# A hybrid decoder layer on one core: the order of sampled tokens' state steps, the spacing of the second up set, and a feature-major last quarter

## The chip, the cores and the metric

The kernel runs on one core of a Trainium2 chip. The core has a matrix engine (TensorE, PE in the profile, with its weight loads as PEld), a vector engine (VectorE, DVE), an activation engine (ScalarE, ACT), a general engine (GpSimd, POOL) and a queue that issues transfers (SyncE, SP). Each works through its own instructions in order; between engines there are semaphores. The metric is the time of one execution on the device in microseconds. Before the change it has a median of 1743.32 us in three runs (1743.06 to 1748.29).

## The reference, cut to what matters

One layer for 1024 new tokens and 8 sampled tokens (one each for 8 sequences with stored state), width 1024, all in float32:

- A norm, and one input projection of 6672 columns, split into queries, forget gates, values and gates of a gated recurrence with 8 heads (HGRN2), and gate z, x/B/C and time steps of a state-space mixer with 16 heads (Mamba-2).
- HGRN2 by chunks; the mixer by chunks of 128 with a state of 64 x 128 a head. For a sampled token the stored state is decayed, `S = S * exp(A dt) + (dt x) B`, and read, `y = S C + D x`.
- Both are normed, gated, joined and multiplied by `w_out`, and added to x.
- A norm, `w_up` to 2 x 2816 columns, a causal convolution of width 3 on the gate half, `silu(gate) * val`, `w_down`, added to x. A last norm follows:

```python
gate, val = jnp.split(h @ w['w_up'], 2, axis=-1)
x = x + (jax.nn.silu(gate) * val) @ w['w_down']
y = rmsnorm(x, final_norm_w)
```

Returned are the normed outputs, both recurrent states of both groups, and the convolution states.

## The kernel before, in words

Every large product is made of three matmuls: each operand is split into a rounded part (`hi`) and the rest (`lo`), and hi x hi, hi x lo and lo x hi are added up in PSUM. A split is a cast on ScalarE and a difference on VectorE, for weights (L199 and L201, L1443 and L1444) as for activations (L1344 and L1345).

Activations lie feature-major: 128 features on the partitions, tokens along the row. Weights are loaded by SP some tiles ahead. The PSUM pool "mm" has three banks, the pool "mx" four, and there is one "nx".

The order of TensorE's instructions is written out by hand up to the last round of the down product: a list of jobs (one weight tile each: `f`, `q`, `v`, `sg`, `z`, `x`, `o`) is driven one matmul at a time (`step`, `tick`), and smaller work is put between them. `after(n, work)` issues work n ticks later, `spread(pieces, n)` issues one piece every n ticks. On the other engines a planner sets the order: it takes what is ready by its own estimate of times, and of several ready instructions the one issued first in the program. Each engine then runs the planned order, whatever the true times are. `tc.issue_after(ins)` makes an instruction stand behind `ins` on its engine.

Three places matter here.

The state-space mixer: `drive(ssd(1), ...)` runs the second half of the heads beside jobs up to `v0`. `ssd_back` ends a chunk with the state's update on VectorE (L611), and `ssm_state_out` (L633) transposes the last state on TensorE (L636), copies it on VectorE (L638) and stores it. Later, at the beginning of the jobs z4, z5 and z6, `ssm_decode(0, i)` (L656) makes two half steps for the sampled tokens of one pair of heads: SP loads B, C and the stored state Sd, ScalarE scales Sd (L669, four instructions), VectorE makes the product with B (L670) and adds it (L671), SP stores it, POOL multiplies by C (L673), VectorE reduces (L674). Before z4 come the four jobs of head 0, `f0`, `q0`, `v0`, `sg0`, whose PSUM tiles ScalarE evicts at L926. The buffers of Sd (two, tag "ld") and of B and C (four, tag "d") are used by head 0 next (L959 to L964).

The up product: instead of the plain product, each up tile takes seven products of half depth (p1 to p7) on combinations of the blocks of activations and of weights (a Strassen-Winograd scheme). The tokens come as two sets, `usets[0]` and `usets[1]`. `set_of(1)` (L1320) builds the second: its pieces are splits (`put`) and combinations (`comb`, on VectorE or POOL, L1352), issued one every 6 ticks while the first up tile's products run on set 0. It pauses until every feature tile has been weighed (`weigh`, ScalarE, L1257). The norm's factor is applied to products later; `set_norm` computes it (L736 to L739) with a PSUM bank of "mx" for one of its parts. `up_load(j)` loads the weights of up tile j, `up_sums(j)` makes their four sums (POOL, L1424), `up_split` splits them. For j = 1 the sums are made only when `set_of(1)` has issued its combinations, and stand on POOL behind the last of them. `Up` evicts the products: ScalarE copies p1 and p5, VectorE adds p2, p4, p6, p7 and p3, POOL makes two differences after p7 (L1479, L1480).

The end: the last two tiles of the down product are done for quarters of the tokens in the order 3, 0, 1, 2. Quarters 3, 0 and 1 are feature-major: eight products of six matmuls (`down`), added to x on VectorE (L1688), then for each block of 128 tokens eight transposes into two "fin" banks of "mx" (L1695), the squares on ScalarE (L1697), the root, and two scalings with the last norm's weight (ScalarE L1704 and POOL L1705 for one half, VectorE L1707 for the other). Quarter 2 is token-major (`last_blocks`, L1657): activations are the stationary operand, the last weights the moving one, 512 wide, the products land in "fin" banks as tokens x features, and x is added by matmuls with the identity on its split halves, which `halved` (L1627) prepares.

Of the kernel before, what the change touches and what calls it, by code (L numbers as in the profile page):

```python
# [16 lines left out]
P = 128  # L17
# [33 lines left out]
def hybrid_layer(  # L51
# [578 lines left out]
    def h64(t):  # L630
        return t.rearrange("p (h q) -> p h q", q=64)

    def ssm_state_out(g):  # L633
        ps = bank("sT")
        for i in range(4):
            PE.transpose(ps[:, i * P:(i + 1) * P], S[g][:, i * P:(i + 1) * P], ident)  # L636
        so = half("so")
        V.tensor_copy(so, ps)  # L638
        SP.dma_start(ssm_prompt[0, 0, g * 8:(g + 1) * 8].rearrange("(i h) p n -> (h p) i n", h=2),
                     so.rearrange("p (i n) -> p i n", n=P))  # L640

    def d4(t):
        return t.rearrange("p (b n) -> p b n", n=P)

    def cb(t):
        return t.unsqueeze(2).to_broadcast([P, 4, P])
# [9 lines left out]
    def ssm_decode(g, i):  # L656
        j = g * 4 + i
        xdd = small.tile([P, 2, ND], F32, tag="xdd", name=nm("xdd"))
        xdec = xdk[:, j, :]
        V.tensor_tensor(xdd[:, 0, :], xdec, ddb[:, 0, j, :], op=ALU.mult)  # L660
        for b0 in (0, 4):
            bs = slice(b0, b0 + 4)
            Bb, Cb = tl("d", "Bb")[:, :512], tl("d", "Cb")[:, :512]
            for t_, r in ((Bb, 2 * g), (Cb, 2 * g + 1)):
                fetch(t_, bc_d[r, bs].rearrange("b n -> (b n)").unsqueeze(0).to_broadcast([P, 512]))
            Sd = tl("ld", "Sd")
            fetch(d4(Sd), state_ssm[0, bs, 2 * j:2 * j + 2].rearrange("b h p n -> (h p) b n"))
            for b in range(4):
                A.activation(d4(Sd)[:, b, :], d4(Sd)[:, b, :], AF.Copy, scale=ddb[:, 1, j, b0 + b:b0 + b + 1])  # L669
            V.tensor_tensor(d4(Bb), d4(Bb), cb(xdd[:, 0, bs]), op=ALU.mult)  # L670
# [243 lines left out]
    def head_in(h):  # L914
        t = {}

        def f_end():
            f, k = t["f"], tl("big" if h else "e", "k")
            A.activation(f[:, :NT], f[:, :NT], AF.Identity, bias=lbt2[:, 0, h:h + 1], scale=lbt2[:, 1, h:h + 1])
            V.tensor_scalar(k[:, :NT], f[:, :NT], -1.0, 1.0, op0=ALU.mult, op1=ALU.add)  # L920
            t["k"] = k

        for n, off, func in (("f", OFF_F, AF.Tanh), ("q", OFF_Q, AF.Silu), ("v", OFF_I, AF.Copy),
                             ("sg", OFF_G, AF.Silu)):
            def evict(c, cs, ps, n=n, func=func):
                A.activation(t[n][:, cs], ps, func, scale=0.5 if n == "f" else 1.0)  # L926
# [388 lines left out]
        mm(ps[:, :QW], ones, rst[:, cs])  # L1315
        rstd_of(rst[:, cs], tl("us", "nt"), ps[:, :QW], DM)

    usets, combed = [{}, {}], [None]

    def set_of(i):  # L1320

# [26 lines left out]
        def comb(out, eng, x_, y_, op):  # L1348
            t = quads(tl("x5", "sm")[:, :NT])
            out.append(t)  # L1350
            for q in range(2):
                combed[0] = eng.tensor_tensor(t[:, 2 * q:2 * q + 2], x_[q], y_[q], op=op)  # L1352
                yield

        def two(t):
# [21 lines left out]
            after(76, lambda: up_split(0, 1))  # L1377
        else:
            d_ = []
            yield from put("p1", a1, "hT")  # L1380
            yield from comb(d_, G, a1, b1, ALU.subtract)
            while len(weighed) < KT:
                yield
            yield from put("p2", a2, "big")
            yield from put("p4", b2, "big")
            yield from comb(s_, V, b1, b2, ALU.subtract)
            yield from comb(s_, V, two(s_[0]), a1, ALU.subtract)
            yield from comb(s_, G, two(s_[1]), a2, ALU.add)
            up_sums(1, combed[0])
            yield from put("p6", [s_[1]], "hT")  # L1390
            yield from put("p5", [s_[0]], "hT")
            yield from put("p7", d_, "hT")
# [7 lines left out]
    def up_load(j):  # L1400
        ws = []
        for c0 in (0, DFF):
# [4 lines left out]
            last_w[0] = SP.dma_start(t.rearrange("p (k m) -> p k m", m=P),  # L1407
                                     w_up[0, :, c0 + j * P:c0 + (j + 1) * P].rearrange("(k p) m -> p k m", p=P))
            ws.append(t)
        wparts[j] = ws  # L1410
        if j != 1:
            up_sums(j)

    def up_sums(j, behind=None):

        (g1, g2), (v1, v2) = ((t[:, :512], t[:, 512:]) for t in wparts[j])
        sums = {}

        def add(name, x_, y_):
            sums[name] = tl("t", "wt")  # L1420
            with ExitStack() as order_:
                if behind is not None:
                    order_.enter_context(tc.issue_after(behind.ins))
                (G if j else V).tensor_tensor(sums[name], x_, y_, op=ALU.add)  # L1424
            return sums[name]

        p7 = add("p7", v1, v2)
# [114 lines left out]
    with tc.manual_schedule(engines={mybir.EngineType.PE}):  # L1542
# [6 lines left out]
            tick()  # L1549
        up_split(0, 2)  # L1550
        up_split(0, 3)
        after(4, lambda: spread(set_of(1), 6))
        after(93, lambda: (set_norm(1, 0), set_norm(1, 1)))
        for _ in ups(0, [(name, i) for i in range(2) for name in FIRST]):
            tick()
# [63 lines left out]
    for k in range(nk):  # L1619
# [5 lines left out]
    halves_ = []  # L1625

    def halved():  # L1627
        identr = tl("us", "idr", F32R)[:, :P]
        A.copy(identr, ident)
        halves_.append(identr)  # L1630
        for h4 in range(2):
            hi, lo = tl("x5", "xfh", F32R)[:, :1024], tl("x5", "xfl", F32R)[:, :1024]
            halves_.append((hi, lo))
            for m in range(4):
                x_, at_ = xT[4 * h4 + m][:, quarters[2]], slice(m * 256, (m + 1) * 256)
                A.copy(hi[:, at_], x_)
                V.tensor_tensor(lo[:, at_], x_, hi[:, at_].bitcast(F32), op=ALU.subtract)
                yield

    def summed(b):  # L1640
        t0 = quarters[2].start + b * P
        tb = [bank("fin"), bank("fin")]
        for i in range(2):
            ds, first_ = slice(i * 512, (i + 1) * 512), True
            for k in range(nk):
                for a, x in ((0, 0), (1, 0), (0, 1)):
                    mm(tb[i], acts[k][a][:, t0:t0 + P], wd[k][x][:, ds], start=first_, stop=k == nk - 1 and x == 1)
                    tick()
                    if first_:
                        first_ = False  # L1650
                        for m in range(4):
                            for x_ in halves_[1 + i]:
                                mm(tb[i][:, blk[m]], x_[:, m * 256 + b * P:m * 256 + (b + 1) * P], halves_[0],
                                   start=False, stop=False)
        return t0, tb

    def last_blocks():  # L1657
        for b in range(2):
            t0, tb = summed(b)
            ss = keep.tile([P, 4], F32, tag="ss", bufs=4, name=nm("fss"))  # L1660
            ot, sq = ([tl("t", "ot") for _ in range(2)] for _ in range(2))
            for i in range(2):
                ds = slice(i * 512, (i + 1) * 512)
                A.activation(sq[i], tb[i], AF.Square, accum_out=ss[:, i:i + 1])
                V.tensor_tensor(ot[i], tb[i], fw[:, ds], op=ALU.mult)
            V.tensor_tensor(ss[:, 2:3], ss[:, 0:1], ss[:, 1:2], op=ALU.add)
            A.activation(ss[:, 3:4], ss[:, 2:3], AF.Sqrt, bias=epsc, scale=1.0 / DM)
            V.reciprocal(ss[:, 3:4], ss[:, 3:4])
            for i in range(2):
                if i:  # L1670
                    A.activation(ot[i], ot[i], AF.Copy, scale=ss[:, 3:4])
                else:
                    V.tensor_scalar(ot[i], ot[i], ss[:, 3:4], None, op0=ALU.mult)
                SP.dma_start(y_prompt[0, t0:t0 + P, i * 512:(i + 1) * 512], ot[i])

    for c in (3, 0, 1, 2):
        cs = quarters[c]
        if c == 2:
            for _ in split_:
                pass  # L1680
            last_blocks()
            break
        if c == 0:
            split_ = halved()
            spread(split_, 3)
        for m in range(KT):
            ps = down(lambda k: wd[k], nk, slice(m * P, (m + 1) * P), acts, c)
            V.tensor_tensor(xT[m][:, cs], xT[m][:, cs], ps, op=ALU.add)  # L1688
        for t0 in range(cs.start, cs.stop, P):
# [10 lines left out]
            V.reciprocal(ss[:n, 3:4], ss[:n, 3:4])  # L1700
            for i in range(2):
                ds = slice(i * 512, (i + 1) * 512)
                if i:
                    A.activation(ot[i][:n], tb[i][:n, :], AF.Copy, scale=ss[:n, 3:4])  # L1704
                    G.tensor_tensor(ot[i][:n], ot[i][:n], fw[:n, ds], op=ALU.mult)  # L1705
                else:
# [33 lines left out]
```

## Time and profile before

| | |
|---|---|
| median of three runs | 1743.32 us |
| profiled execution, its time | 1742.79 us |
| its span, first to last instruction | 1741.1 us |
| TensorE busy | 1705.4 us, 98% of the span |
| VectorE, ScalarE, POOL busy | 1089.1, 789.8, 483.4 us |
| mean granted clock of TensorE | 0.997 |

Rows of the timeline give the start and the duration in us, the engine, the line of the kernel, the operation and its tiles (out<-in). In brackets stands how long the engine was idle before it and what ended that. A row "A <- B: t, n, m" of the waits says that A waited for B for t us in n waits, the longest m. Rows of stretches give, for A:B us, the length, each engine's busy time with its count, the granted clock, the DMA share and GB/s.

### The profile page before, as it was taken

The page shows a single profiled execution, that of the slowest core. Times are in us where ns is not written, and L with a number is a line of the kernel's source. Part 1 is how long each engine was busy: PE and PEld are TensorE (multiplying, and loading weights), DVE is VectorE, ACT ScalarE, POOL GpSimd, SP SyncE. Part 2 cuts the span into 40 slices and gives each one's busy share as a digit, 9 for nine tenths or more (in the row PEclk, how much of TensorE's full clock was granted, in tenths as well). Part 3 has the DMA queues.
Part 4 walks back from the last instruction along what each step waited for, and adds up shares of the span by engine and source line. Part 5 has one row for each costly group of instructions (what it writes and reads, how often), then busy time and mean ns, then how long its engine had stood idle before and what let it go on. Part 6 is the DMA issues. An engine that isn't in the chain of part 4 may idle for free. (4 is left out here: it accounts for less than half of the span.)

```text
span 1741.1 us, 38505 instructions
## 1 busy us (share of the span) xinstructions
PE 1705.4 (98%) x16111; PEld 1656.5 (95%) x16111; DVE 1089.1 (63%) x1983; ACT 789.8 (45%) x1441; POOL 483.4 (28%) x501
## 2 busy tenths in 40 slices
PE   7999999999999999999999989999999999999998
PEld 7999999999999999999999989999999999999997
DVE  6668666555565565567746777667676668544454
ACT  7677686344454354545334554333344334111124
POOL 2102131110120122011222266666666664000002
PEclk9999999999999999999999999999999999999999
DMA  5354334633434425335347712222222226322212
GB/s 165 73 123 120 96 91 144 186 103 105 130 94 120 115 88 142 118 99 178 119 145 252 230 53 87 97 74 74 74 80 80 97 75 240 138 90 77 86 44 98
DMA packets 250212, 200.22 MB, mean 115 GB/s; under 512 B 48020, under 2 KB 221574, under 8 KB 250022
## 3 DMA queue, kind: packets, MB, share of 16 engines
q1 hardware_dynamic: 249750, 197.67, 37.2%
q8 instruction: 126, 2.06, 0.5%
q14 instruction: 48, 0.39, 0.1%
q0 software_dynamic: 288, 0.10, 0.0%
HBM read 155.16 MB, written 46.95 MB: 116 GB/s over the span
## 5 line engine op out<-in xcount | busy, mean ns | idle before, releaser
L93 PE MATMUL mm<-hl,wh 128*128 128x344 f32 x1248 | 405.5, 325 | 0.0
L93 PE MATMUL mm<-hh,wh 128*128 128x344 f32 x1248 | 405.0, 325 | 0.0
L93 PE MATMUL mm<-hh,wl 128*128 128x344 f32 x1248 | 402.0, 322 | 0.0
L93 PEld LDWEIGHTS mm<-hl,wh 128*128 128x128 f32 x1248 | 235.4, 189 | 4.8 <-issue 4.2
L93 PEld LDWEIGHTS mm<-hh,wh 128*128 128x128 f32 x1248 | 235.4, 189 | 3.4 <-issue 2.8
L93 PEld LDWEIGHTS mm<-hh,wl 128*128 128x128 f32 x1248 | 235.6, 189 | 1.4 <-issue 1.2
L199 ACT CAST wh<-ws 128x1024 fp32r<-128x1024 f32 x96 | 100.6, 1048 | 238.8 <-PE dn L93 125.8
L93 PE MATMUL ub<-uh,wh 128*128 128x258 f32 x704 | 199.7, 284 | 4.1 <-DVE nt L737 3.3
L93 PE MATMUL ub<-uh,wl 128*128 128x258 f32 x704 | 198.9, 283 | 0.0
L93 PE MATMUL ub<-ul,wh 128*128 128x258 f32 x704 | 198.3, 282 | 0.0
L93 PE MATMUL dn<-ah,wh 128*128 128x256 f32 (+1 forms) x640 | 180.6, 282 | 1.1 <-DVE x L1611 1.1
L93 PE MATMUL dn<-al,wh 128*128 128x256 f32 (+1 forms) x640 | 180.2, 282 | 0.0
L93 PE MATMUL dn<-ah,wl 128*128 128x256 f32 (+1 forms) x640 | 179.7, 281 | 0.0
L201 DVE TENSOR_TENSOR wl<-ws,wh 128x1024 fp32r<-128x1024 f32 x88 | 115.3, 1310 | 81.0 <-ACT wh L199 81.0
L93 PE MATMUL ua<-uh,wh 128*128 128x258 f32 x528 | 149.6, 283 | 2.6 <-DVE val L1506 1.3
L93 PE MATMUL mm<-mh,wh 128*128 128x258 f32 x512 | 146.3, 286 | 4.9 <-DVE x L1233 4.1
L93 PE MATMUL ua<-uh,wl 128*128 128x258 f32 x528 | 149.3, 283 | 0.1
L93 PE MATMUL ua<-ul,wh 128*128 128x258 f32 x528 | 148.7, 282 | 0.0
L93 PE MATMUL mm<-ml,wh 128*128 128x258 f32 x512 | 145.1, 283 | 0.0
L93 PE MATMUL mm<-mh,wl 128*128 128x258 f32 x512 | 144.7, 283 | 0.0
L93 PEld LDWEIGHTS ub<-uh,wh 128*128 128x128 f32 x704 | 133.0, 189 | 4.5 <-DVE nt L737 3.5
L1444 DVE TENSOR_TENSOR wl<-wt,wh 128x512 fp32r<-128x512 f32 x88 | 89.6, 1037 | 75.1 <-ACT wh L1443 75.0
(394 smaller groups left out, 3982.5 us busy)
## 6 DMA issues: line engine op xcount, KB each, us to landing
ws<-in_w_in_dram SPq DMA_DIRECT2D x52, 512.0 KB
ws<-in_w_up_dram SPq DMA_DIRECT2D x44, 512.0 KB
ws<-in_w_out_dram SPq DMA_DIRECT2D x24, 512.0 KB
act_d<-val SPq DMA_DIRECT2D x22, 516.0 KB
al<-act_d SPq DMA_DIRECT2D x22, 516.0 KB
ws<-in_w_down_dram SPq DMA_DIRECT2D x22, 512.0 KB
ml<-mix_d SPq DMA_DIRECT2D x48, 172.0 KB
csb<-cs_d SPq DMA_DIRECT2D x32, 256.0 KB
```

The source lines that it names most:

```text
L93: PE.matmul(out, lhsT, rhs, start=start, stop=stop)
L199: A.copy(wh[:, :n], ws[:, :n])
L201: V.tensor_tensor(wl[:, :n], ws[:, :n], wh[:, :n].bitcast(F32), op=ALU.subtract)
L1444: V.tensor_tensor(lo[:, cs], sums[name], hi[:, cs].bitcast(F32), op=ALU.subtract)
```

## The change

Four things are changed. `ssm_decode`'s product with B stands on VectorE behind the newest copy of a state (`freed[0]`), and its scaling on ScalarE behind the newest eviction of a head's job (`freed[1]`). At the beginnings of z4, z5 and z6 these are the copy of the second state, L638, and the third eviction of `sg0`. In `set_of(1)` the d combination comes ahead of the p1 splits, the p4 splits come behind the combinations, and a piece is issued every 4 ticks instead of 6. The sums of up tile 1 are made by `up_load`, like all others, with no place given on POOL. Quarter 2 at the end is done like the other three; for it alone both halves are scaled on VectorE. `halved`, `summed` and `last_blocks` go.

```diff
-        V.tensor_copy(so, ps)
+        freed[0] = V.tensor_copy(so, ps)
...
             for b in range(4):
-                A.activation(d4(Sd)[:, b, :], d4(Sd)[:, b, :], AF.Copy, scale=ddb[:, 1, j, b0 + b:b0 + b + 1])
-            V.tensor_tensor(d4(Bb), d4(Bb), cb(xdd[:, 0, bs]), op=ALU.mult)
+                with tc.issue_after(freed[1].ins):
+                    A.activation(d4(Sd)[:, b, :], d4(Sd)[:, b, :], AF.Copy, scale=ddb[:, 1, j, b0 + b:b0 + b + 1])
+            with tc.issue_after(freed[0].ins):
+                V.tensor_tensor(d4(Bb), d4(Bb), cb(xdd[:, 0, bs]), op=ALU.mult)
...
-                A.activation(t[n][:, cs], ps, func, scale=0.5 if n == "f" else 1.0)
+                freed[1] = A.activation(t[n][:, cs], ps, func, scale=0.5 if n == "f" else 1.0)
...
+            yield from comb(d_, G, a1, b1, ALU.subtract)
             yield from put("p1", a1, "hT")
-            yield from comb(d_, G, a1, b1, ALU.subtract)
             while len(weighed) < KT:
                 yield
             yield from put("p2", a2, "big")
-            yield from put("p4", b2, "big")
             yield from comb(s_, V, b1, b2, ALU.subtract)
             yield from comb(s_, V, two(s_[0]), a1, ALU.subtract)
             yield from comb(s_, G, two(s_[1]), a2, ALU.add)
-            up_sums(1, combed[0])
+            yield from put("p4", b2, "big")
             yield from put("p6", [s_[1]], "hT")
...
-        wparts[j] = ws
-        if j != 1:
-            up_sums(j)
-
-    def up_sums(j, behind=None):
-
-        (g1, g2), (v1, v2) = ((t[:, :512], t[:, 512:]) for t in wparts[j])
+        (g1, g2), (v1, v2) = ((t[:, :512], t[:, 512:]) for t in ws)
...
-        after(4, lambda: spread(set_of(1), 6))
+        after(4, lambda: spread(set_of(1), 4))
...
     for c in (3, 0, 1, 2):
         cs = quarters[c]
-        if c == 2:
-            for _ in split_:
-                pass
-            last_blocks()
-            break
-        if c == 0:
-            split_ = halved()
-            spread(split_, 3)
...
-                if i:
+                if i and c != 2:
                     A.activation(ot[i][:n], tb[i][:n, :], AF.Copy, scale=ss[:n, 3:4])
                     G.tensor_tensor(ot[i][:n], ot[i][:n], fw[:n, ds], op=ALU.mult)
                 else:
```

More of the change, by code (lines that the diff above doesn't have):

```diff
@@ L631, in h64 @@
         return t.rearrange("p (h q) -> p h q", q=64)
+    freed = [None, None]
     def ssm_state_out(g):
@@ L1316, in set_norm @@
         rstd_of(rst[:, cs], tl("us", "nt"), ps[:, :QW], DM)
-    usets, combed = [{}, {}], [None]
+    usets = [{}, {}]
     def set_of(i):
@@ L1351, in comb @@
             for q in range(2):
-                combed[0] = eng.tensor_tensor(t[:, 2 * q:2 * q + 2], x_[q], y_[q], op=op)
+                eng.tensor_tensor(t[:, 2 * q:2 * q + 2], x_[q], y_[q], op=op)
                 yield
@@ L1420, in add @@
             sums[name] = tl("t", "wt")
[L1421 to L1424, printed above, removed]
+            (G if j else V).tensor_tensor(sums[name], x_, y_, op=ALU.add)
             return sums[name]
@@ L1624, in hybrid_layer @@
         wd.append((hi, lo))
[L1625 to L1669, printed above, removed]
-                if i:
[L1671 to L1674, printed above, removed]
```

1 line of the change is left out of this document (removed).

## The prediction

> **What bounds the kernel now.** I read the page first, then TensorE's own waits, and then the timeline of all queues around the longest of them.
>
> ```profile
> span 1741.1 us, 38505 instructions
> PE 1705.4 (98%) x16111; PEld 1656.5 (95%) x16111; DVE 1089.1 (63%) x1983; ACT 789.8 (45%) x1441; POOL 483.4 (28%) x501
> ```
>
> TensorE is busy for 1705.4 of 1741.1 us, so 35.7 us are left, and the start and the last stores take part of those. An edit can gain only where TensorE stands still or where it takes matmuls away. Its waits, as receiver, releaser, total, count and longest:
>
> ```profile
> PE ub L93 <- DVE nt L737: 3.3, 1, 3.3
> PE sT L636 <- DVE S L611: 2.4, 1, 2.4
> PE fin L93 <- ACT ot L1704: 1.7, 1, 1.7
> PE ua L93 <- DVE val L1506: 1.3, 1, 1.3
> PE ua L93 <- DVE us L1478: 1.0, 1, 1.0
> PE ub L93 <- ACT us L1474: 0.8, 1, 0.8
> ```
>
> Each of the three longest stands in one of the three places that the diff touches. So the question is, place by place, whether the edit takes the wait away and what is late next.
>
> **Part A, sampled tokens beside z4 to z6.** The rows are start, duration, instruction, and in brackets the idle time before it.
>
> ```profile
> 307.69 1.42 DVE L624 SCALAR_TENSOR_TENSOR xbc<-xbc,d_bc,ecs 128x128 f32<-128x128 f32 x4
> 311.18 0.70 DVE L670 TENSOR_TENSOR Bb<-Bb,xdd 128x512 f32<-128x512 f32 x1 [2.07 <-DMA Bb<-bc_d]
> 313.39 0.69 DVE L670 TENSOR_TENSOR Bb<-Bb,xdd 128x512 f32<-128x512 f32 x1 [0.92 <-DMA Bb<-bc_d]
> 314.00 0.68 DVE L611 TENSOR_TENSOR S<-S,st 128x512 f32<-128x512 f32 x1
> 314.74 0.66 PE L636 MATMUL sT<-ident,S 128*128 128x128 f32 x4 [2.44 <-DVE S L611]
> 312.71 1.28 ACT L669 ACTIVATE Sd<-Sd,ddb 128x128 f32<-128x128 f32 x4 [6.80 <-DMA Sd<-in_state_ssm_dram]
> 330.29 0.44 ACT L926 ACTIVATE sg<-mm 128x344 f32<-128x344 f32 x1
> 348.12 0.44 SPq L182 DMA_DIRECT2D Sh<-in_state_hgrn_dram  x1
> 381.82 1.30 POOL L964 TENSOR_TENSOR Sh<-Sh,vb 128x512 f32<-128x512 f32 x1
> 330.00:341.00 11.00, 11.00 (x72) 11.00 (x71) 5.11 (x10) 3.61 (x10) 2.59 (x2) 1.00 0.69 207
> ```
>
> VectorE is in order. Two products of the sampled tokens (L670) stand in its queue ahead of the state's last update (L611) and wait for their loads, 2.07 and 0.92 us, while the transposes of that state (L636) stand on TensorE. With the change both L670 come behind the state's copy, which needs those transposes. VectorE is then free at 307.69 + 1.42 = 309.11; one 0.68 us product (as L611) and L611 itself end at about 310.5, before TensorE reaches the transposes at 314.74 - 2.44 = 312.30. So the whole wait goes: **-2.4 us**. Bounds: -2.4, and 0 if other work of VectorE slips in front of L611 instead.
>
> What is moved: the four copies of each half step on ScalarE (L669) now stand behind the last eviction of the job before z4 (330.29 less 2.4 = 327.9) instead of at 312.71, 15 us later; the products, the store of Sd on SP behind them, POOL's L673 and the loads of the next step, which reuse the buffers, follow. The z5 and z6 steps name that same eviction, so nothing new holds them. Queued behind the copies on ScalarE are evictions of z4 to z6; those copies now find their loads landed (they were issued before 312), where today ScalarE stands 6.80 us for them. A z job is 72 matmuls in 11.0 us without a gap, thus 3.7 us per PSUM bank of three, so an eviction may be about 7 us late before TensorE feels it: two halves of 1.28 us are hidden. SP also brings head 0's states later: 348.12 + 15 = 363, while POOL uses them at 381.82, 18 us of cover. I cost these at nothing; uncovered, each would show as ScalarE's wait for a load.
>
> **Part B, the second set and the sums of the second up weights.**
>
> ```profile
> 1017.85 0.66 POOL L1251 TENSOR_TENSOR n2r<-n2r,n2sq 128x258 f32<-128x258 f32 x1 [0.38 <-ACT n2sq L1250]
> 1021.08 0.69 DVE L1352 TENSOR_TENSOR sm<-sm,x 128x516 f32<-128x516 f32 x1
> 1026.07 1.61 POOL L1479 TENSOR_TENSOR val<-us,us 128x258 f32<-128x258 f32 x1 [7.55 <-issue]
> 1028.34 2.36 POOL L1352 TENSOR_TENSOR sm<-sm,x 128x516 f32<-128x516 f32 x2
> 1030.74 1.05 ACT L1344 CAST uh<-sm 128x1032 fp32r<-128x1032 f32 x1 [5.70 <-POOL sm L1352]
> 1031.82 1.23 DVE L1345 TENSOR_TENSOR ul<-sm,uh 128x1032 fp32r<-128x1032 f32 x1 [2.98 <-ACT uh L1344]
> 1033.78 0.39 PE L93 MATMUL ub<-uh,wh 128*128 128x258 f32 x1 [3.27 <-DVE nt L737]
> 1035.57 1.48 POOL L1424 TENSOR_TENSOR wt<-wt,ws 128x512 f32<-128x512 f32 x1
> L1444 DVE TENSOR_TENSOR wl<-wt,wh 128x512 fp32r<-128x512 f32 x88 | 89.6, 1037 | 75.1 <-ACT wh L1443 75.0
> L1444 DVE TENSOR_TENSOR wl<-ws,wh 128x512 fp32r<-128x512 f32 x66 | 47.7, 723 | 0.0
> ```
>
> The chain behind the 3.27 us: POOL stands 7.55 us in front of L1479, whose input comes late, although the third combination of the second set (POOL L1352) behind it had its input at 1021.08 + 0.69 = 1021.8. ScalarE's split (L1344) waits 5.70 us for that combination, VectorE's (L1345) 2.98 us, and behind it the norm's L737, which holds the bank that TensorE wants.
>
> In the program's order a piece came every 6 matmuls. The pieces go on once all of the second half is weighed, about 28 matmuls in, so the third combination was issued at about 28 + 8 x 6 = 76, after L1479 (the end of the sixth product, 72). Now it is at 28 + 6 x 4 = 52, since the pieces are 4 apart and the p4 splits come after it. It stands ahead of L1479 in the order by which the planner chooses, and can run from 1021.8 to 1021.8 + 2.36 = 1024.2 instead of 1030.7; the split then ends by 1024.2 + 1.05 + 1.23 = 1026.5, and the norm on VectorE is no longer behind a wait: **-3.3 us**. The d combination only changes places with the p1 splits; the same 18 pieces are issued.
>
> The four sums of up weight 1 (POOL, to 1035.57 + 1.48 = 1037.1 today) are issued behind the combinations still, at 72, but are free to go as soon as their weights are there. POOL has a hole of 1026.07 - 1018.51 = 7.6 us after its last L1251; at 1.48 us each they take 5.9 of them. On ScalarE the splits of these sums no longer wait for POOL. The waits of 1.0, 0.8 and 1.3 us listed above come after this place, from VectorE and ScalarE catching up; I leave them in the sum. Bounds of B: -6.4 (all four waits go), and +3.8, if the sums run against VectorE's densest stretch: its L1444 takes 1037 ns beside POOL's sums' operands and 723 ns otherwise, 0.31 us more, on about a dozen instructions. I take -3.3 as the value nearest to the row that the edit names.
>
> The Trainium skill, "SBUF — State Buffer", section "Who interferes with whom", speaks against this edit: a VectorE instruction with two SBUF inputs and a GpSimd instruction that reads SBUF exclude each other, and the second waits for the whole of the first. The 1037 against 723 ns agree with it in kind; they stand for a part of a block, not all of it. Were each of the four sums to hold VectorE once for its full length, B would be -3.3 + 4 x 1.48 = +2.6, inside the bounds above and close to rival 2 below.
>
> **Part C, the end.**
>
> ```profile
> 1538.82 21.29 PE dn L93 x180
> 1706.58 0.43 DVE x L1688
> 1719.98 2.13 PE L1695 MATMUL fin<-ident,x 128*128 128x128 f32 x16
> 1720.10 0.75 DVE L1707 SCALAR_TENSOR_TENSOR ot<-fin,fss,fw 128x512 f32<-128x512 f32 x1
> 1721.65 0.70 ACT ot L1697 x2
> 1722.37 0.17 DVE fss L1698
> 1722.56 0.30 ACT fss L1699
> 1722.89 0.17 DVE fss L1700
> 1723.09 0.70 ACT ot L1704
> 1723.83 11.02 PE fin L93 x56
> 1724.00:1728.00 4.00, 4.00 (x18) 3.35 (x19) 1.07 (x3) 2.69 (x8) 2.46 (x2) 0.65 0.49 183
> 1736.97 0.72 ACT L1671 ACTIVATE ot<-ot,fss 128x512 f32<-128x512 f32 x1 [0.23 <-DVE fss L1668]
> ```
>
> Today the last quarter's 56 matmuls need a "fin" bank that ScalarE frees at 1723.79. TensorE ran transposes from 1719.98 to 1722.11, stood 1.72 us, and then worked at a granted clock of 0.65 over four us: 11.02 us in all, and the last product ends at 1737.69.
>
> The new quarter is 8 x 6 = 48 matmuls at 21.29 / 180 = 0.118 us, 5.7 us, into banks of the "mm" pool, which the transposes do not use. It can begin at 1722.11 and ends at 1727.8. The last addition (0.43) and the transpose behind it end near 1728.6, the other block's eight (2.13 / 2 = 1.06) at 1729.7. From the start of the second square to the start of the scaling today's chain has 1723.09 - 1721.65 = 1.44 us, so the first block's two products on VectorE run from 1730.05 to 1731.55. The second block's squares follow the first's root on ScalarE, at 1729.9 + 2 x 0.70 = 1731.3; 0.74 later its two products start, and end at 2 x 0.75 more, 1733.55. That is 4.1 us before 1737.69. For the planner's order and four stores in quick succession I take off 0.5: **-3.6 us**. Bounds: -4.4, and 0 where ScalarE's squares wait for buffers that earlier stores still hold. The casts and differences of `halved` that vanish lay beside matmuls and are worth nothing.
>
> The row of 0.65 is also where the Trainium skill bears ("TensorE: Matmul & The Clock Gate", parts 1 and 4): the clock halves after an idle window of about 3.4 us, and transposes do not count as busy. It agrees, with 3.85 us from 1719.98 to 1723.83 ahead of the drop; by it the new end, with 2.13 us of transposes, keeps its clock.
>
> **Sum.** -2.4 - 3.3 - 3.6 = -9.3 us on a profiled execution of 1742.79 us (span 1741.1), which is 0.5 below the median of 1743.32: 1733.5 there, 1734.0 as a median. 0.3% of the time is 5.2 us, about what a measurement of this kernel can tell; its limits are 1738.1 and 1748.5.
>
> **Rivals.**
> 1. B's wait stays: the planner still puts L1479 first, because its plan has the input earlier than the 1026.07 of the trace. For it: it has misjudged just this today. Against: the order of issue is turned round. -2.4 - 3.6: 1737.3. Chance 0.18.
> 2. POOL's sums fall on VectorE and evictions of the up products are late: B = +3.8, in all -2.2: 1741.1. For it the 1037 ns; against, the hole of 7.6 us on POOL. Chance 0.14.
> 3. The change does not do what it says in A: L670 moves but other work keeps L611 late, and the transposes still stand: 1736.4. Chance 0.08.
> 4. Slower: the steps, 15 us later, make ScalarE stand for Sd among z4 to z6's evictions. A wait of 6.80 and two halves of 1.28 is 9.4 us; if evictions are late already and only one bank of 3.7 us covers it, TensorE stands 5.7 us in each of three steps, 17 us: 1734.0 + 17 = 1751. It decides from 14.5 us on, 4.8 a step. For it: all six half steps share two Sd buffers. Against: the row of 330 to 341 has no gap on TensorE, with one such step beside a z job, and the first step's loads come early. Chance 0.10.
>
> The forecast has 0.50. Faster: 0.50 and 0.08, and two thirds of rival 1, which straddles 1738.1: 0.70. Same: the rest of it and rival 2, 0.20. Slower: 0.10. The range: down to B at -6.4, 1730.9, and up to rival 2, 1741.1, each rounded outward by half a microsecond; the likeliest case alone has 1730.5 to 1737.
>
> **What would show it.** A: L636 without idle time, L670 after L638, L669 after the last sg eviction, no gap on TensorE from 312 to 341. B: POOL's L1352 ahead of L1479, no wait of "ub" for L737. C: matmuls of the last quarter right behind the transposes, clock 1.00, and some 12 us from the end of those transposes (1722.11 today) to the last product instead of 15.6. Wrong it would be through a wait that today's trace doesn't have: "mm" banks not evicted in z5 to z7, or "ua" and "ub" waiting for L1470 and L1478 in the first up tile.

## The result and the profile after

The changed kernel takes 1738.13 us in the median (1734.56 to 1740.45), the kernel before 1745.31 us on the same chip. The ratio is 0.996 with an interval of 0.9949 to 0.997: it is 5.2 to 8.9 us faster. The forecast of 1734.0 us against a median of 1743.32, 9.3 us less, lies just outside that interval. Its range of 1730.5 to 1741.5 holds the time. The profiled execution took 1735.88 us.

The head of the page of the changed kernel, and those of TensorE's waits that bear on the argument, in the columns used for the kernel before:

```profile
span 1734.2 us, 38519 instructions
PE 1702.0 (98%) x16119; PEld 1655.4 (95%) x16119; DVE 1088.9 (63%) x1981; ACT 784.4 (45%) x1430; POOL 483.6 (28%) x501
```

```profile
PE ub L93 <- DVE fext L1488: 2.7, 1, 2.7
PE dn L93 <- DVE x L1605: 2.2, 2, 1.3
PE yo L93 <- DVE S L611: 0.6, 1, 0.6
PE ua L93 <- DVE val L1500: 0.4, 1, 0.4
```

The waits "sT" (2.4) and "fin" (1.7) are gone. "ub" is still there, shorter by 0.6 us and with another releaser: no longer the norm's line but L1488, the eviction of the first up tile's fourth product. The small waits of 1.0 and 0.8 us behind it are gone, and that for `val` fell from 1.3 to 0.4. A second wait for "dn" is new.

**Part A.** The timeline of the changed kernel at the second state's transposes (its L674 is L670 before, its L672 is L669):

```profile
311.41 0.67 DVE L611 TENSOR_TENSOR S<-S,st 128x512 f32<-128x512 f32 x1
313.93 0.60 PE L638 MATMUL sT<-ident,S 128*128 128x128 f32 x4
314.56 0.69 DVE L640 COPY so<-sT 128x512 f32<-128x512 f32 x1 [0.65 <-PE sT L638]
316.31 1.28 DVE L674 TENSOR_TENSOR Bb<-Bb,xdd 128x512 f32<-128x512 f32 x2
327.06 2.44 ACT L672 ACTIVATE Sd<-Sd,ddb 128x128 f32<-128x128 f32 x8
```

A window behind the transposes of the changed kernel, and then the stall and what follows it in the kernel before (length, busy time of the five engines, granted clock, share of DMA, GB/s). The odd bounds are the clock's own steps; the last section explains them:

```profile
316.00:318.00 2.00, 2.00 (x15) 2.00 (x14) 1.59 (x3) 0.67 (x1) 0.00 (x0) 1.00 0.61 163
```

```profile
312.09:315.50 3.41, 0.97 (x8) 0.77 (x7) 2.49 (x5) 1.88 (x6) 0.00 (x0) 1.00 0.61 205
315.50:318.92 3.42, 3.42 (x14) 3.42 (x13) 3.42 (x7) 3.25 (x6) 1.32 (x1) 0.50 0.27 77
```

L611 comes ahead of the products, which start at 316.31 behind the copy L640, and ScalarE's eight copies stand at 327.06 and find their loads there. Behind the stall, the kernel before worked at half the clock for 3.4 us; the changed kernel stays at 1.00. Set beside each other by the same matmul, the two executions differ by +1.04 us at 306 (that arose by 40 us, ahead of everything that the change touches) and -2.40 at 320. So A gained 3.4 us in these two traces, of which the prediction priced 2.4.

**Part B.** The timeline of POOL, VectorE and TensorE at the first up tile, changed kernel:

```profile
1014.03 2.61 DVE L1349 TENSOR_TENSOR ul<-x,uh 128x516 fp32r<-128x516 f32 x2
1022.32 1.20 POOL L1356 TENSOR_TENSOR sm<-sm,x 128x516 f32<-128x516 f32 x1 [1.30 <-DVE sm L1356]
1024.61 3.51 DVE L1349 TENSOR_TENSOR ul<-sm,uh 128x1032 fp32r<-128x1032 f32 x3
1028.04 0.41 DVE L1472 TENSOR_TENSOR us<-us,ua 128x258 f32<-128x258 f32 x1
1028.37 1.22 DVE L1349 TENSOR_TENSOR ul<-sm,uh 128x1032 fp32r<-128x1032 f32 x1
1028.62 1.56 POOL L1473 TENSOR_TENSOR val<-us,us 128x258 f32<-128x258 f32 x1 [5.10 <-DVE us L1472]
1029.52 0.41 DVE L1488 TENSOR_TENSOR fext<-us,ub 128x258 f32<-128x258 f32 x1
1029.98 0.39 PE L93 MATMUL ub<-uh,wh 128*128 128x258 f32 x1 [2.72 <-DVE fext L1488]
```

The stretch with that stall, and the one behind it:

```profile
1027.34:1030.75 3.41, 0.77 (x6) 0.77 (x7) 2.58 (x4) 2.11 (x6) 2.13 (x2) 1.00 0.00 0
1030.75:1034.17 3.42, 3.42 (x18) 3.39 (x18) 3.26 (x9) 1.15 (x2) 0.13 (x1) 0.50 0.00 0
```

The third combination (L1356) does run ahead of L1473, as forecast, and ScalarE's 5.7 us wait is gone. But four differences of the set (L1349, 4.7 us together) now stand in VectorE's queue in front of or between L1472 and L1488, and L1488 frees the bank that TensorE wants. The clock falls behind this stall. It had stayed at 1.00 behind the 3.27 us of the kernel before, but in that trace alone. In the traces of A alone, C alone and the products alone (below), which have the old set, the same wait was 3.32 to 3.36 us, and half the clock followed for 3.41, 6.83 and 6.83 us. It cost nothing that shows there: the same matmuls, from 1005 to 1066 in the kernel before, take 60.5 to 60.8 us with it and 61.0 without, and the small waits behind it are fewer.

**Part C.** The timeline at the end of the changed kernel, and the window from 1726 on:

```profile
1716.64 2.29 PE L1630 MATMUL fin<-ident,x 128*128 128x128 f32 x16
1724.75 1.91 PE L1630 MATMUL fin<-ident,x 128*128 128x128 f32 x16
1729.79 1.41 DVE L1642 SCALAR_TENSOR_TENSOR ot<-fin,fss,fw 128x512 f32<-128x512 f32 x2
```

```profile
1726.00:1730.00 4.00, 0.66 (x7) 0.42 (x4) 2.18 (x7) 2.28 (x9) 0.00 (x0) 1.00 0.26 96
```

From the end of the first transposes (1718.93) to the last product (1731.20) are 12.3 us; the prediction had said some 12 instead of 15.6. From 1711 to the end of the span the changed kernel gains 3.9 us.

The second wait for "dn", at the first additions of the down projection, has these rows in the timeline of the changed kernel:

```profile
1467.89 1.22 DVE L1158 TENSOR_TENSOR al<-al,ah 128x1032 fp32r<-128x1032 f32 x1
1469.04 1.08 DVE L1605 TENSOR_TENSOR x<-x,dn 128x256 f32<-128x256 f32 x3
1469.50 0.39 PE L93 MATMUL dn<-ah,wh 128*128 128x256 f32 x1 [0.91 <-DVE x L1605]
```

A difference of the next round's activations (L1158) stands ahead of additions that free banks. No line of the diff is there; the planner ordered it anew. It costs 1.3 us between 1460 and 1480.

### The profile page after: what moved, and what is told of

Its sections match the earlier page's. It is cut to its first block, busy times and chain, and to the rows that moved or that the text cites. A ratio compares the mean times of both kernels' runs of the same rounds, so it can differ in the third digit from the quotient of the medians.

```text
span 1734.2 us, 38519 instructions
## 1 busy us (share of the span) xinstructions
PE 1702.0 (98%) x16119; PEld 1655.4 (95%) x16119; DVE 1088.9 (63%) x1981; ACT 784.4 (45%) x1430; POOL 483.6 (28%) x501
## 5 line engine op out<-in xcount | busy, mean ns | idle before, releaser
L1438 DVE TENSOR_TENSOR wl<-wt,wh 128x512 fp32r<-128x512 f32 x88 | 90.1, 1043 | 75.9 <-ACT wh L1437 75.9
```

The lines of the kernel that those rows point to most:

```text
L1438: V.tensor_tensor(lo[:, cs], sums[name], hi[:, cs].bitcast(F32), op=ALU.subtract)
```

## Experiments

Gains are given against the kernel before, as the ratio's distance from 1 times the median before, with the interval behind it. The diffs are cut to the lines that matter.

### Each part alone

The first kernel has only the diff's lines with `freed`, the second only those of the set and the sums, the third only the new end.

> The kernel before with part A alone: the sampled tokens' copies and products ordered behind the newest eviction and the second state's copy; the second set, the sums and the end as before. Theory (the parts are independent, and A is worth its stall and the clock drop that came with it): the wait at the transposes of the second state falls from 2.4 to below 0.7 us, the clock of 314 to 320 us stays at 1.00 instead of 0.50 to 0.88, the state's transposes begin about 1 us earlier relative to the matmuls before them, and the whole kernel is 3.5 to 4.3 us faster than before, about 1739 on a profile of 1742.8. The 3.27 us wait of the second set and the 1.7 us wait of the end are there as before. Rival (only the stall counts, the clock drop moves elsewhere): 2.0 to 2.6 us faster. Rival (what A frees is lost at the next late buffer): within 1 us of before.

> The kernel before with part B alone: pieces of the second set 4 matmuls apart, in the new order, and the sums of the second up weights with their load; the sampled tokens and the end as before. Theory (the 5.7 us wait of ScalarE for POOL goes, but the evictions of the first up tile stand behind the set's differences on VectorE, so that a wait of some 2.7 us with the opposite sign takes its place, and only the three small waits behind it are won): 1.5 to 2.8 us faster than before. Rival (the first wait that was left in the changed kernel comes of A, which shifted VectorE's work at that place): the wait does not appear here and it is 4 to 6 us faster. Rival (B is worth nothing by itself): within 1 us.

> The kernel before with part C alone: the last quarter feature-major like the others, its two scalings on VectorE. Theory: the 1.7 us wait for a bank and the clock of 0.65 from 1724 on are gone, the last quarter's matmuls run at 1.00, and it is 3.2 to 4.0 us faster than before; nothing ahead of 1700 us changes by more than 0.5 us. Rival (the clock was already low for the end because of earlier transposes, so the new end shows a drop too): 1 to 2.5 us faster.

Measured: A alone 0.9972 (0.9961 to 0.9983), 4.9 us (3.0 to 6.8). B alone 0.9988 (0.9977 to 0.9999), 2.1 us (0.2 to 4.0). C alone 0.9987 (0.9978 to 0.9996), 2.3 us (0.7 to 3.8). They add up to 9.3 us. The whole change had 7.0 (5.2 to 8.9), and in the later comparison below 9.1 (6.5 to 11.9). So the parts are independent within what can be told, and no part is seen to eat another's gain.

A's theory of 3.5 to 4.3 us lies inside the measured interval, and both its rivals lie outside. B alone shows the wait of 2.73 us behind the fourth product's eviction too, so A does not cause it, and its gain is the theory's. C alone fell short of its theory (2.3 us where 3.2 to 4.0 were expected, though its interval reaches 3.8), and something did change ahead of 1700.

C alone brings the same second "dn" wait (0.90 us), and the kernels of A or B alone don't have it: it belongs to C. Between 1460 and 1480 C's kernel loses 1.6 us to the kernel before, and from 1711 on it wins 4.0. The size of A is less sure. In B's and C's kernels, which have the transposes' order of before, the stall was shorter; the timeline of B's:

```profile
315.50 0.66 PE L636 MATMUL sT<-ident,S 128*128 128x128 f32 x4 [1.91 <-DVE S L611]
```

It is 1.91 us there and 1.66 in C's, and in both the clock stayed at 1.00 behind it. The matmuls from 306 to 320 in the kernel before take 14.0 us in its trace, 11.9 and 11.6 in B's and C's, and 9.7 to 11.1 (10.4 in the mean) in the ten traces with the products moved. The 3.4 us above thus owe much to one execution; the means differ by 2.1 us. The measured 3.0 to 6.8 us reach further, and what makes up the rest was not found.

### One half of A

Against the kernel with A alone:

```diff
-                with tc.issue_after(freed[1].ins):
-                    A.activation(...)
+                A.activation(...)
```

> The kernel before with one half of part A: the products on VectorE ordered behind the second state's copy, while ScalarE's copies stay where the planner puts them. Theory (the stall of the transposes came of VectorE's products alone): no stall at the transposes of the second state, the clock at 1.00 there, and a time within 1.5 us of the kernel with the whole of part A, 3 to 5.5 us faster than before. Rival (the copies on ScalarE, left in front of the evictions of z3, make the next wait): a wait for sg's or z's bank of 1 us or more between 312 and 335, and at most 2.5 us faster than before.

Measured: 0.9984 (0.9971 to 0.9996), 2.8 us (0.7 to 5.1). The stall of the transposes is gone, and another stands 30 us later in its timeline. That is the rival's mechanism, but later than the stretch that it named (312 to 335):

```profile
344.01 1.28 ACT L671 ACTIVATE Sd<-Sd,ddb 128x128 f32<-128x128 f32 x4
345.19 1.03 ACT L199 CAST wh<-ws 128x1024 fp32r<-128x1024 f32 x1
346.13 0.45 ACT L763 ACTIVATE sz<-mm 128x344 f32<-128x344 f32 x1
346.63 0.42 PE L93 MATMUL mm<-hh,wh 128*128 128x344 f32 x1 [1.92 <-ACT sz L763]
```

With the products later and the copies not, ScalarE has four copies of a later step and a weight split ahead of an eviction. By the same matmul this kernel is 3.1 us ahead at 320 and 0.3 at 350. In the whole of part A the copies stand behind an eviction, and from 318 to 350 the timeline lists no gap of TensorE. The prediction had costed the copies' move at nothing. The trace puts it at 2.8 us; the two kernels differ by 2.1 us (4.9 less 2.8), but their intervals overlap, so the size is not shown.

### What sets the wait at the first up tile

Four kernels, each the changed kernel with one edit. The first holds the last pieces of the set behind the eviction:

```diff
+            while i and name in ("p5", "p7", "p3") and not sums_up:
+                yield
...
+                    if i and name in ("p5", "p7", "p3"):
+                        order_.enter_context(tc.issue_after(sums_up[0].ins))
```

> The changed kernel with the last six pieces of the second set (p5, p7, p3) held until the first up tile's fourth product is evicted, and their differences on VectorE ordered behind that eviction; nothing else differs. Theory (the eviction was late only because three differences of the set stood ahead of it in VectorE's queue): the wait of 2.7 us at the first up tile and the clock of 0.50 to 0.69 behind it are gone, and it is 3 to 4.5 us faster than the changed kernel, thus 10 to 11.5 us faster than before. Rival (VectorE is short of time over the whole stretch, its work stretched by POOL's sums beside it, so that the order only decides who waits): the wait stays between 1.5 and 3 us or moves to the products that use p5, p7 and p3, and it is within 1.5 us of the changed kernel, 6 to 8.5 us faster than before.

Measured: 0.9964 (0.9952 to 0.9976), 6.3 us (4.2 to 8.4): no faster than the changed kernel, as its rival had it. In its timeline the eviction is early and the wait is longer:

```profile
1025.58 0.42 DVE L1493 TENSOR_TENSOR fext<-us,ub 128x258 f32<-128x258 f32 x1
1025.92 4.47 DVE L1354 TENSOR_TENSOR ul<-sm,uh 128x1032 fp32r<-128x1032 f32 x3
1030.65 0.75 DVE L741 SCALAR_TENSOR_TENSOR nt<-n2ms,n2r 128x258 f32<-128x258 f32 x2
1031.45 0.39 PE L93 MATMUL ub<-uh,wh 128*128 128x258 f32 x1 [3.37 <-DVE nt L741]
```

The differences were moved in front of the next instruction that frees a bank, the norm's L741. The second edit puts p7 and p3 behind the norm as well:

```diff
+            behind = {"p5": sums_up, "p7": normed, "p3": normed}.get(name) if i else None
...
-        after(93, lambda: (set_norm(1, 0), set_norm(1, 1)))
+        after(93, lambda: (set_norm(1, 0), normed.append(set_norm(1, 1))))
```

> The changed kernel with p5's difference held behind the eviction of the first up tile's fourth product, and p7's and p3's held behind the last instruction of the second set's norm (the line that ended the wait when only the eviction was put first). Theory (VectorE has the time; what counts is that everything that frees a PSUM bank stands ahead of differences that are used 6 us later): no wait of TensorE over 1.3 us between 1005 and 1045, the clock stays at 1.00, and it is 3 to 4.5 us faster than the changed kernel, about 10 to 11.5 us faster than before. Rival (VectorE has no time left in this stretch): the wait moves once more, to the products that use p7 and p3 or to the next evictions, with at least 2 us in all, and the time is within 1.5 us of the changed kernel.

Measured: 0.9947 (0.9932 to 0.9961), 9.2 us (6.8 to 11.9). The wait is 1.2 us, with the clock at 1.00. That fits the theory on the place, but not its size: against the changed kernel the same matmuls gain 1.9 us between 1020 and 1045 and give 1.3 back by 1066. A wait of 0.7 us for one of the held differences (L1355) is new, and the wait for `val` is 1.6 us, 1.3 before the change. With the 1.2 us that makes 3.5 us, over the 2 us that the rival had named for waits that move on. The time lies between the two expectations, and its interval overlaps that of the changed kernel.

The third edit takes work off VectorE instead, the differences of p7 and p3 to POOL:

```diff
-                V.tensor_tensor(lq[:, rows], t, hq[:, rows].bitcast(F32), op=ALU.subtract)
+                (G if i and name in ("p7", "p3") else V).tensor_tensor(
+                    lq[:, rows], t, hq[:, rows].bitcast(F32), op=ALU.subtract)
```

> The changed kernel with the two last differences of the second set, p7 and p3, on POOL instead of VectorE, the order of the rest as it is. That takes 2 x 1.22 us off VectorE between 1024 and 1031 and puts some 2 x 2.4 us on POOL, which stood from 1022.9 to 1028.6. Theory (VectorE is the bound of the stretch): the 2.7 us wait shrinks to below 1.5 us, without a drop of the clock, and it is 2.5 to 4 us faster than the changed kernel. Rival (POOL's two-input work slows VectorE's beside it, and POOL's product and difference of the seventh product are now late): the wait stays at 2 to 3.5 us with another name behind it, and the time is within 1.5 us.

Measured: 0.9962 (0.995 to 0.9974), 6.6 us (4.5 to 8.7): nothing gained, and the wait is 3.0 us, as the rival had it. Its timeline:

```profile
1024.13 2.85 POOL L1349 TENSOR_TENSOR ul<-sm,uh 128x1032 fp32r<-128x1032 f32 x1 [1.77 <-ACT uh L1348]
1025.37 2.70 DVE L1349 TENSOR_TENSOR ul<-sm,uh 128x1032 fp32r<-128x1032 f32 x1
1030.54 0.39 PE L93 MATMUL ub<-uh,wh 128*128 128x258 f32 x1 [3.00 <-DVE nt L741]
```

A difference that VectorE does in 1.22 us alone takes 2.70 beside POOL's, and POOL's next product is late. The fourth edit holds POOL's sums of the second up weights behind the third combination, as before the change:

```diff
-            (G if j else V).tensor_tensor(sums[name], x_, y_, op=ALU.add)
+            with ExitStack() as order_:
+                if j == 1:
+                    order_.enter_context(tc.issue_after(combed[0].ins))
+                (G if j else V).tensor_tensor(sums[name], x_, y_, op=ALU.add)
```

> The changed kernel with POOL's four sums of the second up weights held behind the third combination, as they were before the change; the pieces' order and spacing stay. Theory (the sums beside VectorE's differences cost it some 2 to 3 us between 1007 and 1016, 1.44 against 0.89 and 2.61 against 1.29 in two of its instructions): VectorE's instructions of 1010 to 1017 are back at 0.89 and 1.3, the 2.7 us wait is 1.5 us or less, and it is 2 to 4 us faster than the changed kernel, unless the splits of the sums are then late for the second tile. Rival (VectorE's lag at 1026 comes of the set's pace, not of the sums): the wait stays within 0.5 us of 2.7 and the time within 1 us of the changed kernel.

Measured: 0.996 (0.9948 to 0.9972), 7.0 us (4.9 to 9.1), the changed kernel's own time. Its timeline:

```profile
1011.54 1.29 DVE L1349 TENSOR_TENSOR ul<-x,uh 128x516 fp32r<-128x516 f32 x2
1021.54 6.78 DVE L1349 TENSOR_TENSOR ul<-sm,uh 128x1032 fp32r<-128x1032 f32 x3
1022.73 2.28 POOL L1421 TENSOR_TENSOR wt<-ws,ws 128x512 f32<-128x512 f32 x1
1030.18 0.52 PE L93 MATMUL ub<-uh,wh 128*128 128x258 f32 x1 [5.18 <-DVE fext L1491]
```

Each expectation is right in half. Two differences that took 2.61 us beside the sums take 1.29 without them, so the sums do slow VectorE. But they now run beside the three large differences, which take 6.78 instead of 3.51 us, and the wait is 5.18. That the sums cost VectorE time is shown; where they stand only decides which instruction pays.

The same matmuls, from 1005 to 1066 in the kernel before, tell what each order is worth, in one execution each. The four kernels with the old set take 60.5 to 61.0 us. The new set takes 58.8 and 59.6 (two executions of the changed kernel), 59.1 (B alone) and 58.8 (eviction first). With two differences on POOL it is 60.6, with the sums held 60.4. The three kernels with p5 behind the eviction and p7 and p3 behind the norm (two of them follow below) take 58.2, 57.5 and 58.6. So the new set brings some 1.6 us here, and the best order some 1 us more. Putting the evictions first helps, but the rival is right that VectorE runs out of time: from 1018 to 1043 it is busy for 20.6 us before the change, 23.3 after it, and in the kernel with all edits (the third busy time) for nearly all of the 25 us:

```profile
1018.00:1043.00 25.00, 22.64 (x177) 21.34 (x176) 24.96 (x37) 13.20 (x22) 13.41 (x15) 1.00 0.08 23
```

### Two more edits on top

The first lets the next round's activations load and split from the fourth addition of the down projection on. The second changes the order of POOL's two instructions after the seventh product.

```diff
-            nxt = [act_load(r0 + RND + k) for k in range(min(RND, FT - r0 - RND))]
+            nxt = None
...
+                        if nxt is None and c == 3:
+                            nxt = [act_load(r0 + RND + k) for k in range(min(RND, FT - r0 - RND))]
```

```diff
-            G.tensor_tensor(self.val[:, self.at(1)], self.f, self.u3, op=ALU.subtract)
             G.tensor_tensor(self.u2, self.f, self.u2, op=ALU.subtract)
+            G.tensor_tensor(self.val[:, self.at(1)], self.f, self.u3, op=ALU.subtract)
```

> The kernel with p5 behind the eviction and p7 and p3 behind the norm, and beside that the next round's activations loaded and split from the fourth addition of the down projection on, so that VectorE's difference of the split stands behind the additions that free banks at 1466 to 1470. Theory (the second wait of 0.9 us there came of the difference ahead of the additions): one wait of some 1.1 us or none is left there, and it is 0.5 to 1.5 us faster than the kernel with p5, p7 and p3 held alone. Rival (the later loads make a later round wait): a new wait for an activation's load after 1480, and it is slower than that kernel.

> The kernel with p5, p7, p3 and the next activations held, and POOL's two instructions after the seventh product changed in order, so that the difference which the next eviction on VectorE reads comes first. Theory (the 1.2 us that are left at the first up tile are VectorE standing 0.64 us for POOL in front of that eviction, with the norm behind it): that idle time goes, the wait shrinks to 0.4 to 0.8 us and the time is 0.3 to 1 us below that of the kernel without it, which three to five rounds can hardly tell; the profile decides. Rival: the wait is set by the difference of p5 ahead of it, and stays at 1.0 to 1.3 us.

Measured: the first 0.9938 (0.9926 to 0.995), 10.8 us (8.7 to 12.9), and both together 0.9933 (0.9918 to 0.9949), 11.7 us (8.9 to 14.3), a median of 1733.34. With the first, no wait for "dn" is left between 1455 and 1480, and from 1460 to 1480 it gains 2.7 us on the changed kernel, more than the 0.5 to 1.5 expected. With the second, the norm comes right behind the eviction and TensorE waits 0.51 us, but 1.5 us for `val` and 0.7 for L1355 still. In the time, its effect can't be told. The timeline of the kernel with both:

```profile
1028.57 0.41 DVE L1506 TENSOR_TENSOR val<-us,ua 128x258 f32<-128x258 f32 x1
1028.90 0.75 DVE L741 SCALAR_TENSOR_TENSOR nt<-n2ms,n2r 128x258 f32<-128x258 f32 x2
1029.70 0.39 PE L93 MATMUL ub<-uh,wh 128*128 128x258 f32 x1 [0.51 <-DVE nt L741]
```

### The changed kernel again

> The changed kernel once more, for a direct comparison with the kernels of this study. Every theory: 0.996 of the kernel before within its interval, thus 5.2 to 8.9 us faster. Its second profile tells which waits belong to the order of the instructions (there again: 2.7 us at the first up tile, 0.9 us as the second wait of the down projection) and which to the moment (the 0.6 us of the state's products before 310, the waits of 0.3 to 2 us between 800 and 935).

Measured beside the kernel with all edits: 1735.86 us, 0.9948 (0.9932 to 0.9963). The median of the kernel with all edits is 2.5 us below it, and the two intervals overlap. So that all edits together beat the kernel before is shown, and that they beat the changed kernel is likely. The waits of 2.7 us for "ub" and the second for "dn" came again: they belong to the order. The one for "yo" came again too, with 0.5 us. But kernels with the same part A have 0.2 to 1.1 us there, and three of them none over 0.15, so it is of the moment, as expected. The span of this execution was 1740.3, though, 6.1 us more than in the other one. Most of that came in one place: a stall of 1.96 us that ends at 819.89, in the first of these stretches:

```profile
817.86:821.27 3.41, 1.45 (x12) 1.38 (x12) 2.59 (x3) 0.52 (x2) 1.60 (x2) 1.00 0.39 105
821.27:824.68 3.41, 2.71 (x133) 2.34 (x132) 2.28 (x4) 1.60 (x4) 0.00 (x0) 0.50 0.18 47
824.68:828.10 3.42, 3.42 (x17) 3.42 (x17) 3.14 (x7) 2.17 (x5) 0.00 (x0) 0.50 1.01 324
```

The clock is at half for 6.8 us, and between 800 and 830 it lost 4.5 us to the other execution of the same kernel. A span of one execution can therefore not settle 3 us; the ratios can, and the traces say where.

## Why the prediction was right and wrong

The forecast of faster holds, at 5.2 to 8.9 us in the first comparison and 6.5 to 11.9 in the second, against 9.3. That the sum came near is partly luck: judged by the kernels with one part alone, A was put 2.5 us too low, B and C 1.2 and 1.3 too high. The prediction's list of TensorE's waits leaves out longer ones (6.2 us at the start, 1.8 for "xp"); they lie outside the diff and came again, so nothing hangs on it.

- **A (-2.4).** The step holds: L611 ahead of the products, no stall, no cost at z4 to z6, and rival 3 and rival 4 did not come. Two terms were missed. The half clock behind the stall stood in the trace and was not priced: 3.41 us at 0.50 lose 1.7 us. With the 2.4 and less a new wait of 0.6 us ("yo"), that is the 3.4 us, in this execution. And ScalarE's copies were put at nothing, where the kernel with the products alone makes their later place worth about 2 us. Measured: 4.9 (3.0 to 6.8), more than these terms explain.
- **B (-3.3).** This is the step that failed. The combination does come ahead of L1479, so rival 1's reason is refuted (that its 1737.3 lies nearest to the measured 1738.13 is chance), but the conclusion "the norm on VectorE is no longer behind a wait" is not the same as the bank being free in time. VectorE stood for 2.98 us in front of that norm only because of POOL; given its inputs earlier, it has 4.7 us of differences in its queue ahead of L1472 and L1488. I asked what the removed wait would free and not what else would fill that queue. Rival 2 named this place, with POOL's sums and late evictions. That the sums slow VectorE is shown by 2.61 against 1.29 us and 6.78 against 3.51. That they make the evictions late in the changed kernel is not: POOL stands idle there from 1023.5 to 1028.6, while the differences hold VectorE. Rival 2's sign is wrong, since the small waits of 1.0, 0.8 and 0.9 us behind the place went, which I had left in the sum. Measured: 2.1 (0.2 to 4.0), the bounds of +3.8 and -6.4 hold.
- **C (-3.6).** From 1711 on it gained 3.9 us in the changed kernel and 4.0 alone. The clock stayed at 1.00, as forecast. What the sum lacked is 250 us ahead of the end: the planner's new order at 1466 takes 1.3 to 1.6 us back. Measured: 2.3 (0.7 to 3.8).

The difference of 1.22 us that took 2.70 beside POOL overlapped POOL's by 1.61 us (1025.37 to 1026.98) and lost 1.48. The prediction had taken 0.31 us for such a pair, from averages over a whole line. The Trainium skill ("SBUF — State Buffer", "Who interferes with whom") has the second of such a pair wait for the whole of the first: this pair agrees with it, and the 3.27 us lost over some 5.7 of overlap with the held sums are part of a block.

## What to carry over

When a wait is taken away, list what the freed engine will do in its place, in the order of its queue, and put everything that frees a PSUM bank ahead of work whose result is used later. One such move only hands the wait to the next bank (3.37 us here). All of them together took it to 0.51, with 1.5 and 0.7 us of other waits behind it, and some 1 us was won in the stretch: by then VectorE had no time left, and order alone cannot make up for that. And price a stall with the clock behind it (1.7 us a step where TensorE sets the pace, nothing that showed where VectorE did), and an edit at the end also by what the planner reorders elsewhere.

## What the runs showed that was not expected

The clock drop behind a stall is not set by the stall's length alone. In the trace of before, 3.27 us at 1030 left the clock at 1.00. With p7 and p3 on POOL, 3.00 us did too, and a stall of 1.74 us at 1057 then brought 0.50. Stalls of 1.96, 2.44 and 2.72 us were each followed by 3.4 to 6.8 us at 0.50, and those of 1.66, 1.91 and 1.92 by none.

Where a stall falls tells them apart. In each trace the drops begin whole multiples of 3.41 us apart, and those ahead of the idle end last one or two such steps. Cut into stretches on that grid, the 3.27 us of the kernel before lie in two of them, and each has more work of TensorE (the first busy time) than the 0.97 and 0.77 us ahead of the drops shown above:

```profile
1028.89:1032.31 3.42, 1.61 (x14) 1.41 (x12) 0.49 (x1) 1.57 (x3) 3.34 (x4) 1.00 0.00 0
1032.31:1035.72 3.41, 1.94 (x16) 1.94 (x17) 3.41 (x5) 1.70 (x5) 3.41 (x3) 1.00 0.00 0
1035.72:1039.13 3.41, 3.35 (x27) 3.14 (x27) 3.41 (x6) 3.00 (x6) 1.33 (x1) 1.00 0.00 0
```

Take the stretches of all 13 traces from 20 to 1726 us that begin at full clock. Each of the 12 with 1.45 us of work or less was followed by half the clock, and none of those with 1.71 or more. Of seven between, with 1.55 to 1.69 us, five were. A drop lasted a second step where its first was not full of work (2.0 to 2.7 us). So in these runs about half a stretch without work brings the drop, and a stall of 3.3 us can be spared while one of 1.7 is not. Transposes are work in this count: the changed kernel's 1723.66 to 1727.07 has 3.00 us, only 1.25 of it other than transposes, and the clock stays. The prediction had them not count, and took the 3.85 us ahead of the drop at the old end as agreeing; on the grid, the stretch ahead of that drop has 1.69 us of work.

The Trainium skill ("TensorE: Matmul & The Clock Gate", part 1) has a window of about 3.4 us that runs freely, and half the clock after an idle one. The spacing of 3.41 us agrees with it; that the window must be idle does not, by the 1.45 us above. All this is read from the traces: no run moved a stall against the grid, so the bound is not shown by an experiment.
